# Nine gate/up chunk pairs of a feed-forward layer with Strassen's seven products over half of their k-tiles

## The chip, the cores and the metric

The kernel runs on one core of one Trainium2 chip. The metric is the device time of one execution in microseconds; the time of a kernel is the median of its runs. A core has four compute engines that matter here, each with an instruction queue of its own that it works through in order: TensorE (PE in the profile, its weight loads PEld), VectorE (DVE), ScalarE (ACT) and GpSimd (POOL). SyncE (SP) issues the DMA transfers. TensorE reads SBUF and writes PSUM; VectorE and ScalarE read and write both.

## The reference

One decoder layer, 256 rows of 2048 columns, all in fp32:

```python
def swiglu(x, w_in, w_out):
    a, u = jnp.split(x @ w_in, 2, axis=-1)
    return (jax.nn.silu(a) * u) @ w_out

x = layer_norm(ALPHA * x + 0.5 * swiglu(x, ffn1_w_in[i], ffn1_w_out[i]), ln_g[i, 0], ln_b[i, 0])
z = x @ mix_w_in[i]
...
x = layer_norm(ALPHA * x + merged @ mix_w_out[i], ln_g[i, 1], ln_b[i, 1])
x = layer_norm(ALPHA * x + 0.5 * swiglu(x, ffn2_w_in[i], ffn2_w_out[i]), ln_g[i, 2], ln_b[i, 2])
ple = jax.nn.sigmoid(x @ ple_w_gate[i]) * (p[i] @ ple_w_proj[i])
x = layer_norm(ALPHA * x + ple, ln_g[i, 3], ln_b[i, 3])
```

`w_in` is 2048 x 11008: 5504 gate columns (a), then 5504 up columns (u). `w_out` is 5504 x 2048. Between the two feed-forward layers stands a mixer of a short convolution and a gated recurrence (`hgrn`), which the change doesn't touch.

## The kernel before, in words

**Matmuls in three passes.** TensorE works with operands in fp32r. To keep fp32 accuracy each operand is split into a high half (a cast to fp32r) and a low half (what the cast lost), and a product is the sum of three matmuls: high x high (L741), high x low of the weight (L742), low x high (L743). The activations are the stationary operand, in blocks of 128 x 128 (`xh`, `xl` for x; `gh`, `gl` for h); the weights stream as 128 x 512 (`wh`, `wl`). There are two row tiles (t = 0 and 1, 128 rows each), and 16 k-tiles of 128 in a contraction over 2048.

**Units and the ring of weights.** The work is a list of Units (L50): one column block of 512 of one weight matrix, its k-tiles grouped in twos (an element: two k-tiles of 512 columns), the elements grouped in blocks (SPLIT, two blocks of 4 elements for 16 k-tiles). For each block TensorE goes through the elements for t = 0 and then for t = 1. Every element of the whole kernel is in `plan` (L655), in the order of use. `weight_dma` (L668) loads it into a ring of four raw tiles through SP's queue; `weight_split` (L678) makes the high half on ScalarE (L687) and the low half on VectorE (L689, waiting for L687). The halves lie in a ring of six pairs (`NMAIN`), to which each stage can add more (`EXTRA`, L32: four in feed-forward stage 1, three in stage 2). A slot is free again when TensorE has used its element for t = 1. `feed` (L693) is called then and traces as many loads and splits as there is room for.

**What sets the order.** Each use of an element is a tick (L118). Work behind a Unit is deferred by a number of ticks (`defer`) and is traced between matmuls when its tick comes. The framework then schedules the traced program: each engine's final order is made by list scheduling with a simulated timeline, so it can differ from the order of the code; semaphores follow from data, and from the slots of the rings.

**A feed-forward stage** (`ffn`, L293) has three parts over the 5504 hidden columns: 16, 16 and 11 blocks of 128. In a part, each chunk of 512 columns (the last has 384) takes two Units, gate and up. Behind the gate, ScalarE makes SiLU (L305); behind the up, VectorE multiplies (L309) into `h`. h is then transposed, since the next matmul contracts over its columns: `to_stat_blocks` (L204) does it with 16 VectorE instructions on 32-row strips (L202), and `halves` (L182) makes its high half on ScalarE (L189) and its low half on VectorE (L190). At the end of a part four output Units (512 columns of `w_out` each, the part's k-tiles) add into x (L319, L322).

**Normalization.** `layer_norm` (L256) normalizes x, transposes it on TensorE (`transposed`, L176: four matmuls with the identity into one PSUM bank), applies scale and shift on ScalarE (L267) and splits it for the next stage. The same scale and shift are applied to x itself later, by VectorE, column by column at 40, 60, 80 and 100 ticks (L250, L251).

**PSUM** has eight banks: four for accumulators, two for transposes, two for the recurrence.

Of the kernel before, what the change touches and what calls it, by code (L numbers as in the profile page):

```python
# [31 lines left out]
EXTRA = {"ffn1": 4, "hgrn": 0, "merge": 0, "ffn2": 3, "ple": 1}  # L32
# [5 lines left out]
class Stat:  # L38
# [6 lines left out]
    def get(self, t, k):  # L45
        h, l = self.parts[t, k // 4]
        return h[:, k % 4, :], l[:, k % 4, :]


class Unit:  # L50


    def __init__(self, stat, w, row, nk, col, width, epi, split=SPLIT):
# [4 lines left out]
        for n in split:  # L58
            end = min(nk, k + n)
            if k < end:  # L60
                self.blocks.append([list(range(i, min(end, i + KG))) for i in range(k, end, KG)])
            k = end


@with_exitstack
def hybrid_layer(ctx: ExitStack, tc: tile.TileContext, x, p, ln_g, ln_b, ffn1_w_in, ffn1_w_out, mix_w_in,
# [15 lines left out]
    region = {}  # L82

    def open_region(kind):
# [4 lines left out]
        region["kind"] = kind  # L89
        region["pool"] = region["ctx"].enter_context(tc.tile_pool(name=kind, bufs=1, side="left", reuse_waits="tile"))  # L90

# [3 lines left out]
    ps_a = pool("ps_a", 4, space=PSUM)  # L95
    ps_t = pool("ps_t", 2, space=PSUM)
    ps_h = pool("ps_h", 2, space=PSUM)
# [78 lines left out]
    def transposed(src, nb):  # L176
        tp = ps_t.tile([P, CC], F32, tag="tp", name="tp")
# [4 lines left out]
    def halves(stat, t, g, src, nb, tag):  # L182

        where, bufs = (region["pool"], 4) if tag == "m" else (op, 8)
# [19 lines left out]
    def to_stat_blocks(stat, t, g, src, nb, tag):  # L204
        y = rtile([P, 4, P], F32, tag="hT", name="hT", bufs=2)
        turn_blocks(y, src, nb)
        halves(stat, t, g, y[:, :nb, :].rearrange("p a b -> p (a b)"), nb, tag)

# [47 lines left out]
    def layer_norm(t, i, scale, stat):  # L256
# [3 lines left out]
        def operand(c, xc):  # L260
            y = st.tile([P, CC], F32, tag="silu", name="y", bufs=2)
            tp = transposed(xc, 4)
# [6 lines left out]
            halves(stat, t, c, y, 4, "x")  # L269

        for c in range(4):
# [21 lines left out]
    def ffn(xs, w_in, w_out, ln_i, nxt):  # L293
        parts = [(0, 16), (16, 16), (32, 11)]
        for pi, (k0, nk) in enumerate(parts):
            g = Stat()
            ff0 = k0 * P
            ncols = nk * P
            for ci, c0 in enumerate(range(0, ncols, CC)):
                w = min(CC, ncols - c0)  # L300
                silu = {}

                def epi_a(t, acc, silu=silu, w=w):
                    silu[t] = st.tile([P, CC], F32, tag="silu", name="silu", bufs=2)
                    nc.scalar.activation(silu[t][:, :w], acc, AF.Silu)  # L305

                def epi_u(t, acc, silu=silu, w=w, ci=ci, g=g):
                    h = st.tile([P, CC], F32, tag="h", name="h", bufs=3)
                    nc.vector.tensor_tensor(out=h[:, :w], in0=silu[t][:, :w], in1=acc, op=ALU.mult)  # L309
                    defer(2, lambda: to_stat_blocks(g, t, ci, h, w // P, "g"))  # L310

                units.append(Unit(xs, w_in, 0, 16, ff0 + c0, w, epi_a, split=(LONG if ln_i else EARLY) if pi + ci == 0 else SPLIT))
                units.append(Unit(xs, w_in, 0, 16, DFF + ff0 + c0, w, epi_u))
            for c in range(4):
                def epi_o(t, acc, c=c, pi=pi):
                    settle(c)
                    xc = xt[t][:, c * CC : (c + 1) * CC]
                    if pi == 0:
                        nc.vector.scalar_tensor_tensor(out=xc, in0=xc, scalar=2.0 * ALPHA, in1=acc,  # L319
                                                       op0=ALU.mult, op1=ALU.add)  # L320
                    else:
                        nc.vector.tensor_tensor(out=xc, in0=xc, in1=acc, op=ALU.add)  # L322
                    if pi == 2:
                        ln_stat(t, c)
                        if c == 3:
                            layer_norm(t, ln_i, 0.5, nxt)
# [454 lines left out]
```

## Time and profile before

| | |
|---|---|
| Median of 3 runs | 2254.53 us (2253.58 to 2255.19) |
| The profiled execution | 2255.39 us |
| Its span, from the first to the last instruction | 2253.7 us |
| Granted TensorE clock, mean | 0.998 |
| DMA | 429.99 MB, mean 191 GB/s |

All numbers of the trace come from the one profiled execution. A group of instructions is shown as line, engine, operation, output<-inputs, shapes and count, then busy time and mean ns of one, then the idle time of the engine just before them and what ended it. A timeline row has start, duration and the instructions. TensorE's matmuls overlap, so the time that one takes of the engine is the spacing of starts, not its duration. Feed-forward stage 1 runs until about 713 us, the recurrence stage and the merging follow, and feed-forward stage 2 lies between about 1420 and 2135 us.

### The profile page before, as it was taken

How to read it: one execution, taken by the hardware profiler on the slowest of the kernel's cores; microseconds unless marked ns; L12 is line 12 of the kernel's file. 1: busy time of each engine (PE TensorE's matmuls, PEld its weight loads, DVE VectorE, ACT ScalarE, POOL GpSimd, SP SyncE). 2: the span in 40 equal slices, each digit the busy share in tenths (PEclk: the TensorE clock that was granted, in tenths of full speed). 3: DMA queues.
4: the chain of work that ended last, by engine and by line, in shares of the span. 5: the costliest groups of instructions: out<-in, count | busy, mean ns of one | idle time of the engine just before them, and what ended most of it. 6: DMA issues, size and time to landing. Idle time of an engine off the chain costs nothing.

```text
span 2253.7 us, 27116 instructions
## 1 busy us (share of the span) xinstructions
PE 2228.8 (99%) x10154; PEld 1858.6 (82%) x10154; DVE 1498.5 (66%) x2214; ACT 1002.6 (44%) x1168; POOL 9.8 (0%) x32
## 2 busy tenths in 40 slices
PE   9999999999999999999999999999999999999997
PEld 7888888888897888888888888788888888889886
DVE  6776466764685578557555875678745767467667
ACT  6443344433445544434444443644434444344473
POOL 1000000000000000000000000000000000000000
PEclk9999999999999999999999999999999999999999
DMA  8566655566564555554555665566665655655574
GB/s 287 187 203 197 197 186 192 183 207 203 164 197 145 185 181 171 182 180 150 187 187 187 198 199 191 169 214 205 214 199 184 196 192 195 198 190 178 163 242 148
DMA packets 225335, 429.99 MB, mean 191 GB/s; under 512 B 13740, under 2 KB 22452, under 8 KB 225204
## 3 DMA queue, kind: packets, MB, share of 16 engines
q1 hardware_dynamic: 225204, 428.27, 58.7%
q8 instruction: 79, 1.29, 0.2%
q14 instruction: 52, 0.43, 0.1%
HBM read 426.12 MB, written 2.10 MB: 190 GB/s over the span
## 4 chain that ended last, share of the span: by engine, by line
PE 96%; DVE 2%; DMA 1%; ACT 0%; issue 0%; SPq 0%; DVEq 0%; ACTq 0%
PE acc L741 31%; PE acc L743 31%; PE acc L742 31%; PE gp L424 1%; PE tp L179 1%; DVE wl L689 1%; DMA raw<-in_ple_w_gate_dram 0%; DVE x L273 0%; DVE x L286 0%; DVE x L287 0%; DMA x<-in_x_dram 0%; PE dg L394 0%; ACT y L267 0%; DVE xl L190 0%; ACT L224 0%
## 5 line engine op out<-in xcount | busy, mean ns | idle before, releaser
L689 DVE TENSOR_TENSOR wl<-raw,wh 128x1024 fp32r<-128x1024 f32 (+2 forms) x804 | 958.9, 1207 | 500.8 <-ACT wh L687 466.0
L687 ACT CAST wh<-raw 128x1024 fp32r<-128x1024 f32 (+2 forms) x804 | 831.2, 1038 | 1003.8 <-PE acc L743 862.9
L743 PE MATMUL acc<-wh,xl 128*128 128x512 f32 (+1 forms) x2240 | 865.8, 387 | 2.6 <-DVE xl L190 2.6
L741 PE MATMUL acc<-wh,xh 128*128 128x512 f32 (+1 forms) x2240 | 865.5, 388 | 2.2 <-ACT xh L189 2.2
L742 PE MATMUL acc<-wl,xh 128*128 128x512 f32 (+1 forms) x2240 | 865.2, 387 | 0.0
L743 PEld LDWEIGHTS acc<-wh,xl 128*128 128x128 f32 x2240 | 420.8, 188 | 86.3 <-DVE xl L190 4.5
L741 PEld LDWEIGHTS acc<-wh,xh 128*128 128x128 f32 x2240 | 421.0, 188 | 84.1 <-ACT xh L189 3.2
L742 PEld LDWEIGHTS acc<-wl,xh 128*128 128x128 f32 x2240 | 420.9, 188 | 82.1 <-DVE wl L689 0.5
L743 PE MATMUL acc<-wh,gl 128*128 128x512 f32 x880 | 342.5, 389 | 0.0
L741 PE MATMUL acc<-wh,gh 128*128 128x512 f32 x880 | 342.4, 389 | 0.0
L742 PE MATMUL acc<-wl,gh 128*128 128x512 f32 x880 | 342.2, 389 | 0.0
L202 DVE STREAM_TRANSPOSE hT<-h 32x128 f32<-32x128 f32 (+1 forms) x704 | 210.8, 299 | 9.8
L743 PEld LDWEIGHTS acc<-wh,gl 128*128 128x128 f32 x880 | 165.2, 188 | 34.3
L742 PEld LDWEIGHTS acc<-wl,gh 128*128 128x128 f32 x880 | 165.2, 188 | 34.2
L741 PEld LDWEIGHTS acc<-wh,gh 128*128 128x128 f32 x880 | 165.2, 188 | 34.0
L309 DVE TENSOR_TENSOR h<-silu,acc 128x512 f32<-128x512 f32 (+1 forms) x44 | 29.6, 672 | 53.5 <-PE acc L743 53.5
L189 ACT CAST gh<-hT 128x512 fp32r<-128x512 f32 (+1 forms) x48 | 29.5, 614 | 62.8 <-DVE hT L202 62.8
L305 ACT ACTIVATE silu<-acc 128x512 f32<-128x512 f32 (+1 forms) x44 | 25.8, 586 | 52.2 <-PE acc L743 52.2
L322 DVE TENSOR_TENSOR x<-x,acc 128x512 f32<-128x512 f32 x32 | 21.8, 683 | 31.6 <-PE acc L743 31.6
L267 ACT ACTIVATE y<-tp,gbT 128x128 f32<-128x128 f32 x96 | 36.0, 466 | 7.6 <-PE tp L179 4.5
L190 DVE TENSOR_TENSOR gl<-hT,gh 128x512 fp32r<-128x512 f32 (+1 forms) x48 | 32.3, 674 | 0.0
L250 DVE TENSOR_TENSOR x<-x,gb 128x512 f32<-128x512 f32 x24 | 16.4, 723 | 22.0 <-DMA gb<-in_ln_g_dram 22.0
(147 smaller groups left out, 668.6 us busy)
## 6 DMA issues: line engine op xcount, KB each, us to landing
raw<-in_ffn_w_in_dram SPq DMA_DIRECT2D x320, 512.0 KB, 4.7
raw<-in_mix_w_in_dram SPq DMA_DIRECT2D x176, 512.0 KB, 4.6
raw<-in_ffn_w_out_dram SPq DMA_DIRECT2D x168, 512.0 KB, 5.3
raw<-in_mix_w_out_dram SPq DMA_DIRECT2D x32, 512.0 KB, 5.2
raw<-in_ple_w_gate_dram SPq DMA_DIRECT2D x32, 512.0 KB, 5.0
raw<-in_ffn_w_in_dram SPq DMA_DIRECT2D x32, 384.0 KB, 3.9
raw<-in_branch_w_conv_dram SPq DMA_DIRECT2D x16, 512.0 KB, 4.7
raw<-in_branch_w_hgrn_dram SPq DMA_DIRECT2D x16, 512.0 KB, 4.6
```

The costliest lines, as they stand in the source:

```text
L179: state["turned"] = nc.tensor.transpose(tp[:, i * P : (i + 1) * P], src[:, i * P : (i + 1) * P], ident).ins
L189: nc.scalar.copy(hf, src)
L190: nc.vector.tensor_tensor(out=lf, in0=src, in1=hf.bitcast(F32), op=ALU.subtract)
L202: nc.vector.transpose(dst[32 * b : 32 * b + 32, :nb, 32 * q : 32 * q + 32], cols[32 * q : 32 * q + 32, :, b, :])
L267: nc.scalar.activation(y[:, a * P : (a + 1) * P], tp[:, a * P : (a + 1) * P], AF.Identity, bias=gbT[:, 48 + k : 49 + k], scale=gbT[:, k : ...
L305: nc.scalar.activation(silu[t][:, :w], acc, AF.Silu)
L309: nc.vector.tensor_tensor(out=h[:, :w], in0=silu[t][:, :w], in1=acc, op=ALU.mult)
L687: nc.scalar.copy(h[:, :n, :w], raw[:, :n, :w])
L689: nc.vector.tensor_tensor(out=l[:, :n, :w], in0=raw[:, :n, :w], in1=h[:, :n, :w].bitcast(F32), op=ALU.subtract)
L741: nc.tensor.matmul(acc, sh, wh[:, a, : u.width], start=first, stop=False)
L742: nc.tensor.matmul(acc, sh, wl[:, a, : u.width], start=False, stop=False)
L743: nc.tensor.matmul(acc, sl, wh[:, a, : u.width], start=False, stop=last)
```

## The change

It touches the feed-forward stages, the weight rings and the PSUM banks.

**Quads.** Chunks 1 to 9 (nine pairs of gate and up blocks, 512 columns each) are no longer two Units but one Quad. Over the k-tiles 0 to 7 the four blocks (k-tiles `lo` and `hi`, gate and up columns: raw tiles 11, 12, 21, 22) are multiplied with the two row tiles by Strassen's scheme in Winograd's form: seven products instead of eight, with four sums of weight tiles (t1 to t4, made on VectorE in place on the raw tiles before they are split) and four sums of the stationary side (s1 to s4, made once per stage). It is done in two steps of 2 + 2 k-tiles. The k-tiles 8 to 15 stay plain (elements a0, a1 for gate and u0, u1 for up) and are accumulated into the same seven PSUM banks p1 to p7; for this the up columns' first product uses a stationary difference d of the two row tiles. In each step 11 elements are split, where two Units had 8 for the same columns. `after` combines the banks on VectorE and ScalarE: two copies, five additions and subtractions for the up columns, and for each row tile an addition, SiLU and a product.

**Rings.** The raw tiles of the seven products come through a second ring of five tiles (`sraw`, in a pool of its own), the rest through the old one of four. `EXTRA` is 0 in both feed-forward stages, so the ring of split weights has six slots. The cast on ScalarE may be traced one element ahead of the split.

**Order.** The hidden columns are now in five parts (two chunks each, the last has three), and the output Units of a part stand between the chunks of the next: two behind each of its first two chunks. So chunks 1 and 2 follow each other, chunk 2 is followed by two output Units, and so on; chunk 0 and the 384 columns of chunk 10 stay Units, and four output Units of 11 k-tiles end the stage.

**h** is transposed on TensorE (`to_stat`), three ticks after its product, through one PSUM bank. In the feed-forward stages PSUM is divided in seven banks for accumulators and one for transposes; elsewhere as before. The unsplit transposed x of k-tiles 0 to 15 is kept until the stationary sums are made.

```diff
-EXTRA = {"ffn1": 4, "hgrn": 0, "merge": 0, "ffn2": 3, "ple": 1}
+EXTRA = {"ffn1": 0, "hgrn": 0, "merge": 0, "ffn2": 0, "ple": 1}
+NSRAW = 5
+BANKS = {"ffn1": (7, 1, 0), "ffn2": (7, 1, 0)}
...
+class Quad:
...
+        for s in range(2):
+            lo, hi = (2 * s, 2 * s + 1), (4 + 2 * s, 5 + 2 * s)
+            n0, n1 = (8 + 4 * s, 9 + 4 * s), (10 + 4 * s, 11 + 4 * s)
+            k11, k12, k21, k22 = ((self, s, n) for n in ("11", "12", "21", "22"))
+            step = {
+                "11": dict(src=k11, use=[("p1", 0, lo)]),
+                "t1": dict(src=k11, add=k12, use=[("p5", "s1", lo)]),
+                "22": dict(src=k22, use=[("p3", "s4", lo)]),
+                "t3": dict(src=k12, add=k22, use=[("p7", "s3", lo)], free=[k12]),
+                "t2": dict(src=k11, add=k22, use=[("p6", "s2", lo)], drop=[k22]),
+                "21": dict(src=k21, use=[("p2", 0, hi)]),
+                "t4": dict(src=k11, add=k21, use=[("p4", 1, hi)], drop=[k21], free=[k11]),
+            }
+            for n, ks in (("a0", n0), ("a1", n1)):
+                step[n] = dict(load=[(ks, 0)], use=[("p2", 0, ks), ("p4", 1, ks)])
+            for n, ks in (("u0", n0), ("u1", n1)):
+                step[n] = dict(load=[(ks, 1)], use=[("p3", "d", ks), ("p5", 1, ks)])
+            step["11"]["sums"] = [(k12, lo, 1), (k22, hi, 1), (k21, hi, 0), (k11, lo, 0)]
+            order = "11 u0 t1 u1 22 t3 a0 t2 a1 21 t4".split()
...
-            defer((6 if t == 0 else 4) + c, lambda c=c, xc=xc: operand(c, xc))
+            defer((4 if t else 7 if stat is x2 else 6) + c, lambda c=c, xc=xc: operand(c, xc))
...
+        def turn(g, t, ci, h, w):
+            defer(3, lambda: to_stat(g, t, ci, h, w // P, "g"))
...
+                def after(el, ps):
+                    if el["step"] == 0:
+                        return
+                    if el["name"] == "11":
+                        made["c11"] = work("h")
+                        nc.scalar.copy(made["c11"], ps["p1"])
+                    elif el["name"] == "22":
+                        made["c12"] = work("silu")
+                        nc.scalar.copy(made["c12"], ps["p3"])
+                        both(made["c12"], made["c12"], ps["p5"], ALU.add)
+                    elif el["name"] == "t2":
+                        made["e"], made["c22"] = work("silu"), work("h")
+                        e = made["e"]
+                        both(e, made["c11"], ps["p6"], ALU.add)
+                        both(made["c12"], made["c12"], e, ALU.subtract)
+                        both(e, e, ps["p7"], ALU.add)
+                        both(made["c22"], ps["p5"], e, ALU.subtract)
+                    elif el["name"] == "21":
+                        h = made["c11"]
+                        both(h, h, ps["p2"], ALU.add)
+                        nc.scalar.activation(h, h, AF.Silu)
+                        both(h, h, made["c12"], ALU.mult)
+                        turn(g, 0, ci, h, CC)
+                    elif el["name"] == "t4":
+                        e = made["e"]
+                        both(e, e, ps["p4"], ALU.add)
+                        nc.scalar.activation(e, e, AF.Silu)
+                        both(e, e, made["c22"], ALU.mult)
+                        turn(g, 1, ci, e, CC)
...
+        for pi, chunks in enumerate(parts):
+            for ci, ch in enumerate(chunks):
+                in_units(ch, gs[pi], ci)
+                if pi and ci < 2:
+                    out_unit(pi - 1, 2 * ci)
+                    out_unit(pi - 1, 2 * ci + 1)
+        for c in range(4):
+            out_unit(len(parts) - 1, c)
...
+    def weight_cast():
+        el = plan[cur["cast"]]
+        n, w, where = el["n"], el["w"], el["where"]
+        raw = raws[el["src"]]
+        if "add" in el:
+            nc.vector.tensor_tensor(out=raw[:, :n, :w], in0=raw[:, :n, :w], in1=raws[el["add"]][:, :n, :w], op=ALU.add)
+            drop(el.get("drop", ()))
...
+        nc.scalar.copy(h[:, :n, :w], raw[:, :n, :w])
...
     def feed():
         while True:
+            if may_load("sraw"):
+                weight_dma("sraw")
+            elif may_load("raw"):
                 weight_dma()
+            elif castable():
+                weight_cast()
+            elif cur["split"] < cur["cast"]:
                 weight_split()
             else:
                 return
...
+        for el in u.els:
+            for bank, t, ks in el["use"]:
+                tick()
...
+                for a, k in enumerate(ks):
+                    left[bank] -= 1
+                    passes(ps[bank], u.stat, t, k, gi, a, first and a == 0, left[bank] == 0)
+            consumed(gi)
+            u.after(el, ps)
...
+    def first_operand(t, c):
+        tp = transposed(xt[t][:, c * CC : (c + 1) * CC], 4, "a")
+        halves(x0, t, c, tp, 4, "x")
+        nc.scalar.copy(plain_tile(t, c), tp)
+        if (t, c) == (NT - 1, 3):
+            sums(x0)
```

`src` is the raw tile that an element is split from, `add` the one that is added to it first; `use` names bank, stationary operand and k-tiles; `drop` and `free` say which raw tiles are given back after the sum and after the split. `passes` issues the three matmuls per k-tile as before, and `consumed` frees the element's slot and calls `feed`.

More of the change, by code (lines that the diff above doesn't have):

```diff
@@ L82, in hybrid_layer @@
     region = {}
+    held = {}
     def open_region(kind):
@@ L293, in ffn @@
     def ffn(xs, w_in, w_out, ln_i, nxt):
[L294 to L326, printed above, removed]
-                units.append(Unit(g, w_out, ff0, nk, c * CC, CC, epi_o, split=(12,) if (pi == 2 and c == 3) else SPLIT))
@@ L725, in hybrid_layer @@
             feed()
[L726 to L750 removed]
     drain()
     region.pop("ctx").close()
+    region.pop("psum").close()
 _INS = ['x', 'p', 'ln_g', 'ln_b', 'ffn1_w_in', 'ffn1_w_out', 'mix_w_in', 'conv_w', 'hg_lower_bound', 'hg_norm_w',
```

280 lines of the change are left out of this document (214 added, 66 removed).

## The prediction

> **What bounds the kernel now.** I read the page first, then the groups of instructions kept apart by shape, the waits, and the timelines of TensorE and VectorE inside the first feed-forward stage.
>
> ```profile
> span 2253.7 us, 27116 instructions
> ...
> PE 2228.8 (99%) x10154; PEld 1858.6 (82%) x10154; DVE 1498.5 (66%) x2214; ACT 1002.6 (44%) x1168; POOL 9.8 (0%) x32
> ...
> PE 96%; DVE 2%; DMA 1%; ACT 0%; issue 0%; SPq 0%; DVEq 0%; ACTq 0%
> ```
>
> TensorE is busy for 99% of the span and makes up 96% of the chain that ended last. A shorter time needs fewer TensorE instructions, or shorter ones; VectorE, at 66%, has room on average. The average hides where the change puts its work, so the stage counts:
>
> ```profile
> 45.00:713.00 668.00, 668.00 (x2993) 559.00 (x2992) 442.34 (x682) 279.18 (x294) 0.96 (x1) 1.00 0.59 192
> ...
> 840.00:860.00 20.00, 20.00 (x108) 17.13 (x106) 18.06 (x24) 7.87 (x9) 0.00 (x0) 1.00 0.53 163
> ...
> 2000.00:2010.00 10.00, 10.00 (x46) 8.29 (x45) 9.80 (x20) 3.86 (x5) 0.00 (x0) 1.00 0.63 204
> ```
>
> These are answers by stretch: width, then PE, PEld, DVE, ACT, POOL, the granted clock, DMA share, GB/s. The first is feed-forward stage 1: TensorE has no gap in 668 us, the clock is 1.00, VectorE takes 442 us. The other two show VectorE at 90% and 98% for 20 and 10 us while TensorE still has no gap. High VectorE load for a while isn't by itself a stall.
>
> A matmul's mean duration (390 ns) is not its price, since matmuls overlap. The price is the spacing of their starts:
>
> ```profile
> 150.17 0.39 PE L741 MATMUL acc<-wh,xh 128*128 128x512 f32 x1
> ...
> 165.81 0.39 PE L741 MATMUL acc<-wh,xh 128*128 128x512 f32 x1
> ```
>
> Between these two lie 23 rounds of L741, L742, L743: 15.64 us / 69 = 0.2267 us for each.
>
> **Matmuls removed.** A gate/up chunk pair now takes 2 column blocks x 2 row tiles x 16 k-tiles x 3 passes = 192 matmuls. In a Quad, each of its two steps has 7 products of 2 k-tiles, and 4 plain elements of 2 k-tiles used twice: (14 + 16) x 3 = 90, so 180. Nine pairs in two stages: 18 x 12 = 216 fewer, x 0.2267 = **-49.0 us**, all of it on TensorE's path. The output units keep their 43 k-tiles in all, so their matmul count doesn't move.
>
> **Transposes added to TensorE.** h went through VectorE (L202); now it takes four TensorE transposes per 512 columns. The stage after shows what such a group costs:
>
> ```profile
> 768.62 0.39 PE L741 MATMUL acc<-wh,xh 128*128 128x512 f32 x1
> 768.85 0.60 PE L179 MATMUL tp<-ident,s 128*128 128x128 f32 x4
> 769.20 0.48 PE L742 MATMUL acc<-wl,xh 128*128 128x512 f32 x1
> 769.51 0.40 PE L743 MATMUL acc<-wh,xl 128*128 128x512 f32 x1
> 769.75 0.40 PE L741 MATMUL acc<-wh,xh 128*128 128x512 f32 x1
> ```
>
> From L741 to the next L741 pass 1.13 us instead of 3 x 0.2267 = 0.68: a group costs 0.45 us. There are 2 stages x 2 tiles x 11 chunks = 44 groups: **+19.8 us**. The bounds are 0.25 us (if the two matmuls behind it hadn't been slowed) and 4 x 0.272 = 1.09 us (the rows' full duration, below), or 11 to 48 us; I take 0.45 because it is the same operation between the same matmuls. The Trainium skill ("TensorE: Matmul & The Clock Gate", Part 4: PE-mode transpose) speaks against the edit: about 275 ns per transpose in a kernel's context, and the array's full clock isn't held by transposes. By that price the term would be 172 x 0.275 = 47 us and eat nearly all of the gain. The row agrees with the duration but not with the price, since four overlap into 0.45 us, and the granted clock in the stretch 840 to 860 us, which holds small TensorE products, is 1.00.
>
> **VectorE and ScalarE, per Quad.** Rows by shape, and the spacing when they stand back to back:
>
> ```profile
> L689 DVE TENSOR_TENSOR wl<-raw,wh 128x1024 fp32r<-128x1024 f32 x764 | 924.3, 1223 | 482.2 <-ACT wh L687 447.6
> ...
> L687 ACT CAST wh<-raw 128x1024 fp32r<-128x1024 f32 x764 | 799.9, 1050 | 956.2 <-PE acc L743 822.2 <-DMA raw<-in_ffn_w_in_dram 57.4 <-DMA raw<-in_ffn_w_out_dram 26.2
> ...
> L189 ACT CAST gh<-hT 128x512 fp32r<-128x512 f32 x44 | 27.4, 623 | 57.1 <-DVE hT L202 57.1
> ...
> L305 ACT ACTIVATE silu<-acc 128x512 f32<-128x512 f32 x40 | 23.8, 596 | 50.2 <-PE acc L743 50.1
> ...
> L179 PE MATMUL tp<-ident,s 128*128 128x128 f32 x32 | 4.8, 272 | 0.0
> ...
> L389 DVE TENSOR_TENSOR kb<-qT,kT 128x1024 f32<-128x1024 f32 x2 | 2.5, 1226 | 9.8 <-ACT qT L506 9.8
> ...
> L558 ACT COPY b<-acc 128x512 f32<-128x512 f32 x4 | 2.3, 585 | 6.6 <-PE acc L743 6.6
> ```
> ```profile
> 143.93 3.50 DVE L689 TENSOR_TENSOR wl<-raw,wh 128x1024 fp32r<-128x1024 f32 x3
> 147.34 0.68 DVE L309 TENSOR_TENSOR h<-silu,acc 128x512 f32<-128x512 f32 x1
> 147.94 0.68 DVE L190 TENSOR_TENSOR gl<-hT,gh 128x512 fp32r<-128x512 f32 x1
> 148.54 1.22 DVE L689 TENSOR_TENSOR wl<-raw,wh 128x1024 fp32r<-128x1024 f32 x1
> 149.68 5.04 DVE L202 STREAM_TRANSPOSE hT<-h 32x128 f32<-32x128 f32 x16
> ```
>
> Three splits take 3.50 us, so one more costs (3.50 - 1.22)/2 = 1.14; a 512-wide operation costs 0.60 (147.34 to 147.94 to 148.54). A weight sum is the L389 shape (1226 ns against the split's 1223), so also 1.14. A pair before: 16 splits, two products, two times 16 transposes and a low half = 18.2 + 1.2 + 11.3 = 30.7 us of VectorE under 192 x 0.2267 = 43.5 of TensorE. A Quad: 22 splits (25.1), 8 sums (9.1), 9 combining operations (5.4), two low halves (1.2) = **40.8 us**, under 40.8 + 0.9 of TensorE. ScalarE has 22 x 1.05 + 2 x 0.585 + 2 x 0.596 + 2 x 0.623 = 26.7 us. So a Quad alone leaves VectorE nothing. The two output units put behind it bring 8 splits and 4 additions, 11.5 us, under 96 x 0.2267 = 21.8: together 52.3 us of VectorE under 63.5.
>
> What carries work from one to the other is the ring of six split weights; the sums need no ring slot, only their raw tiles, so they can be done early as well. I count from a Quad's start at full TensorE speed (1.36 us for an element used once, 2.72 for one used twice; a step is 20.4). Its first five elements were split while the output unit ran. From there each slot frees when the element six before it ends, and 1.05 + 1.14 us later the next is ready: for the fourth weight sum of the step (element t4) at about 11.7 us, needed at 19.0. The tightest is the next step's first tile, which can only be loaded once that sum has freed a buffer (five buffers in the second ring). The transfer needs:
>
> ```profile
> raw<-in_ffn_w_in_dram SPq DMA_DIRECT2D x320, 512.0 KB, 4.7
> ```
> ```profile
> SPq L674 <- DVE wl L689: 1695.4, 767, 17.5
> ```
>
> The sum ends between 7.5 and 8.9 us, the tile lands 4.7 us later, at 13.6 at the latest, and is split by 15.9; TensorE wants it at 20.4. The margin is 4.5 us. These transfers go through SP's one queue, which already spends 1695 us waiting for splits to free buffers; behind a waiting one stand the raw tiles of elements that are needed later, so this costs nothing while the margin stands.
>
> Two places are tighter. Pairs 1 and 2 follow each other with no output unit between: 81.6 us of VectorE under 83.4. In the second stage the scale-and-shift of the previous normalization falls among them, three of four columns:
>
> ```profile
> 820.39 1.28 DVE L251 TENSOR_TENSOR x<-x,gb 128x512 f32<-128x512 f32 x2
> ...
> 850.72 1.30 DVE L250 TENSOR_TENSOR x<-x,gb 128x512 f32<-128x512 f32 x2 [1.84 <-DMA gb<-in_ln_g_dram]
> ```
>
> That is 3 x 2.6 = 7.8 us more, 6 too much before the ring's store (six elements, some 8 us). I take 3 us there, and 0.2 us for each of the other 16 Quads, where a chain from product over SiLU to transpose ends late: together **+6 us**, from 0 to 18 (1 us a Quad).
>
> Three waits are new. ScalarE's cast of a summed tile waits for the sum; behind it in ScalarE's queue stand the next casts, the SiLUs and the cast of h. TensorE's transposes wait for h, and the next unit's matmuls stand behind them. With one PSUM bank for transposes instead of two, the second group waits until the first is cast and its low half taken (0.62 + 0.60); an element of 1.36 us lies between the two groups, so I put that at nothing, 1 us a Quad (in the 18 us) if VectorE is late.
>
> **The rest.** The second stage's first operands come one tick later: +1.4 us at most, taken. The copies at the start (8 x 0.585 us of ScalarE) lie beside loading of x, and the sums of the stationary side (12 VectorE operations, 7 us) under the first pair, which leaves 43.5 - 19.4: nothing, or 5 us if the cover were gone. The 32 extra additions of the output units are in the counts above. Fewer ring slots (6 for 10 and 9) is what the stage at 840 to 860 us has already.
>
> **Sum.** The profiled execution took 2255.4 us, 1.7 of it outside the span, and 0.9 above the median of the runs, 2254.5. 2255.4 - 49.0 + 19.8 + 6 + 1.4 = 2233.6; less 0.9, **2232.7 us**, 1.0% faster. About 0.2% (4.5 us) is what can be told from no change.
>
> **Rivals.**
> *VectorE becomes the bound in each Quad* (slower). The place is the weight sums: sum, then ScalarE's cast, then split, on the same tile. If VectorE stands idle for the cast, that is 8 x (1.05 + 0.08 of signalling) = 9.0 us, and a Quad needs 49.8. Less what was done ahead (6 x 1.14 and two sums with their idle time, 11.4), plus the next unit's first four (4.6): 43.0 against 41.7, 1.3 us late. In that order the fourth sum comes at 11.6, the next step's tile lands at 16.4, and VectorE, done at 12.7 + 1.14 with it, loses another 3.7 us. 5.0 x 18 = 90 us: 2316. It decides from (49.0 - 19.8 - 1.4)/18 = 1.5 us a Quad. For it: VectorE already waits 447.6 us for casts (row L689). Against it: the order on VectorE isn't the written one. gl (L190) is written straight behind the 16 transposes, yet at 143.93 to 147.94 three splits and a product were put into its wait for ScalarE. The same filling can be done with sums.
> *Transposes at full price*: 0.272 each in the open, 172 x 0.272 = 46.8: 2255.4 - 49.0 + 46.8 + 1.4 - 0.9 = 2253.7, no change. The row at 768.85 speaks against it. It is the price that the page of the Trainium skill named above would give.
> *Better*: no stalls, and transposes at 0.25: 2255.4 - 49.0 + 11 + 0.5 - 0.9 = 2217.
>
> **How the numbers follow.** Forecast 0.64 (2221, with no stall, no late tick and a group at 0.35, to 2250, with 18 us of stall and 5 at the start; 0.02 of it within 0.2%), VectorE bound 0.26 (0.03 of it within, where the stall is near 1.5 us a Quad), transposes at full price 0.06 (0.05 within), better 0.04. So faster 0.66, same 0.10, slower 0.24. The range goes to 2290, about 3.5 us of stall a Quad, which leaves out the upper half of the VectorE case and most of the better one.
>
> **What would show it.** Right: 9,384 weight matmuls for 9,600; 172 transposes of h at about 0.45 us per four; no group of PE with more than some 10 us idle before it; VectorE near 85% in the feed-forward stages and idle in the output units. Wrong: TensorE waiting for weight splits or for h by more than 1.5 us a Quad, VectorE above 95% in a Quad, or casts that wait for the second ring's transfers.

## The result, and the profile after

The changed kernel takes 2266.09 us (median, 2265.55 to 2266.74) where the kernel before took 2254.68 in the same comparison: a ratio of 1.0051, 95% interval 1.0034 to 1.0069. It is slower by 0.5%, where 1.0% faster was forecast. The profiled execution took 2265.55 us, its span is 2263.8 us and its mean granted clock 0.992.

The page of the changed kernel, the same three lines as before:

```profile
span 2263.8 us, 26974 instructions
...
PE 2215.5 (98%) x10110; PEld 1842.7 (81%) x10110; DVE 1682.0 (74%) x1944; ACT 1130.7 (50%) x1331; POOL 10.0 (0%) x32
...
PE 89%; DVE 4%; DMA 3%; ACT 2%; issue 1%; SPq 0%; DVEq 0%; ACTq 0%
```

TensorE's busy time fell by 13 us, and the span still grew by 10. In the chain that ended last TensorE fell from 96% to 89%; VectorE, DMA and ScalarE took its place. TensorE now waits. The stretches say where (columns as in the prediction):

```profile
320.00:340.00 20.00, 20.00 (x90) 16.59 (x89) 19.96 (x21) 12.73 (x14) 0.00 (x0) 1.00 0.76 244
...
120.00:140.00 20.00, 17.96 (x78) 13.75 (x77) 15.65 (x15) 12.51 (x14) 0.00 (x0) 1.00 0.52 164
...
1520.00:1540.00 20.00, 17.63 (x74) 13.00 (x73) 17.64 (x20) 11.53 (x14) 0.00 (x0) 1.00 0.50 135
1540.00:1560.00 20.00, 16.71 (x59) 12.49 (x58) 14.68 (x16) 5.76 (x7) 0.00 (x0) 0.83 0.59 186
...
1400.00:1440.00 40.00, 31.39 (x143) 26.26 (x142) 23.94 (x40) 19.24 (x34) 0.00 (x0) 0.87 0.49 158
```

The first stretch lies in a later Quad: VectorE at 19.96 us of 20, TensorE without a gap. The next three lie in the second Quad of stage 1 and of stage 2 (the end of the first Quad included). There TensorE has gaps while VectorE is *less* busy than in the first; so VectorE isn't simply full, something stops it too. The last is the end of the merging stage.

To count the losses I went over TensorE's rows and added up every spacing of starts beyond what the instruction needs: 0.2267 us for 512 columns, 0.173 for 384, 0.088 for a 128-wide transpose. This is worked out from the rows, not a view of the profile. By place, in us:

| TensorE's loss | before | after |
|---|---|---|
| Start (0 to 40 us) | 6.9 | 11.4 |
| Quads 1 and 2, stage 1 | 0 | 4.5 |
| End of feed-forward stage 1 | 6.6 | 10.3 |
| Recurrence and merging | 6.4 | 6.4 |
| End of merging | 7.0 | 12.9 |
| Quads 1 and 2, stage 2 | 0 | 13.2 |
| Rest of the feed-forward stages | 0 | 4.5 |
| End of feed-forward stage 2 | 1.9 | 7.9 |
| Sum over all spacings | 28.9 | 71.9 |

The rows of the second column make 71.1; the other 0.8 us are a few nanoseconds each in many spacings. The 4.5 us in the rest of the stages are transposes slowing the two matmuls behind them, which the +19.8 us of the prediction hold already. The remaining growth is 71.9 - 28.9 - 4.5 = 38.5 us, and -49.0 + 19.8 + 38.5 = +9.3; behind TensorE's last matmul it is 0.9 longer too, and the span grew by 10.1. So the removed matmuls and the added transposes came as forecast, and three kinds of places ate the gain: Quads 1 and 2 (17.7 us), the stage ends (15.6) and the start (4.5).

Not all of this is waiting. During and behind the waits the granted clock is 0.50 for a while: from 713.5 to 720.2 us, 1427 to 1437, 1553.2 to 1559.9 and 2150.5 to 2153.8, and in the kernel before only behind TensorE's last matmul. The TensorE instructions that start there need about 9 us at the spacings above; as they take twice that, some 9 of the 38.5 us (an estimate from these rows) are the slower clock that comes with the waits.

**Quads 1 and 2.** ScalarE's timeline, then VectorE's, then TensorE's, in stage 2:

```profile
1519.16 1.05 ACT L884 CAST wh<-sraw 128x1024 fp32r<-128x1024 f32 x1 [3.36 <-DVE sraw L878]
1523.80 1.05 ACT L884 CAST wh<-sraw 128x1024 fp32r<-128x1024 f32 x1 [3.58 <-DMA sraw<-in_ffn_w_in_dram]
...
1552.33 1.04 ACT L884 CAST wh<-sraw 128x1024 fp32r<-128x1024 f32 x1 [3.25 <-DMA sraw<-in_ffn_w_in_dram]
```
```profile
1517.86 1.21 DVE L878 TENSOR_TENSOR sraw<-sraw 128x1024 f32<-128x1024 f32 x1
...
1524.87 1.22 DVE L895 TENSOR_TENSOR wl<-sraw,wh 128x1024 fp32r<-128x1024 f32 x1 [2.08 <-ACT wh L884]
...
1546.24 1.22 DVE L878 TENSOR_TENSOR sraw<-sraw 128x1024 f32<-128x1024 f32 x1
...
1553.41 1.22 DVE L895 TENSOR_TENSOR wl<-sraw,wh 128x1024 fp32r<-128x1024 f32 x1 [2.96 <-ACT wh L884]
```
```profile
1553.43 0.80 PE L951 MATMUL p<-wh,xh 128*128 128x512 f32 x1 [2.10 <-ACT wh L884]
```

The fourth sum of a step (L878) ends at 1519.07 us, and only then can the next step's first tile be loaded. The cast of that tile, at the head of ScalarE's queue, waits 3.58 us for the transfer; VectorE, which has to split the tile, stands idle for 2.08 us behind it. One step later the fourth sum ends at 1547.46 us, the cast waits 3.25, VectorE stands idle for 2.96, and TensorE waits 2.10 us for the cast. This is the chain that the prediction's first rival described, fourth sum to next step's tile. In later Quads it is there too, but TensorE has no gap. The row of the waits:

```profile
ACT wh L884 <- DMA sraw<-in_ffn_w_in_dram: 82.9, 20, 5.2
```

Twenty casts waited 82.9 us in all. Most of it cost TensorE nothing: in the fourth Quad of stage 1 the fourth sum ends 9.1 us into its step (235.06 to 244.19) and TensorE goes on without a gap. In the second Quad of stage 1 it ends 18.0 us into the step, in stage 2 22.6. The later Quads have two output units behind them, in which VectorE can catch up.

**Stage ends.** The normalization at the end of merging, on VectorE, in the kernel before and in the changed one:

```profile
1421.33 1.92 DVE L273 TENSOR_SCALAR x<-x,mv,r 128x512 f32<-128x512 f32 x4
1423.16 3.49 DVE L689 TENSOR_TENSOR wl<-raw,wh 128x1024 fp32r<-128x1024 f32 x3
```
```profile
1419.91 1.92 DVE L378 TENSOR_SCALAR x<-x,mv,r 128x512 f32<-128x512 f32 x4
1421.74 4.62 DVE L895 TENSOR_TENSOR wl<-raw,wh 128x1024 fp32r<-128x1024 f32 x4
```

The code holds the next two weight splits back until the normalization of x is through (`gate["lo"]`), to bring the normalization forward. Behind it now stand four splits instead of three, which is all raw tiles there are. The changed kernel's ScalarE, and TensorE:

```profile
1426.71 1.05 ACT L884 CAST wh<-raw 128x1024 fp32r<-128x1024 f32 x1 [4.64 <-DMA raw<-in_ffn_w_in_dram]
1429.32 1.04 ACT L884 CAST wh<-raw 128x1024 fp32r<-128x1024 f32 x1 [1.57 <-DMA raw<-in_ffn_w_in_dram]
1430.27 1.50 ACT L370 ACTIVATE yT<-tp,gbT 128x128 f32<-128x128 f32 x4
```
```profile
1432.47 0.80 PE L951 MATMUL acc<-wh,xh 128*128 128x512 f32 x1 [8.61 <-ACT xh L242]
1433.06 0.63 PE L952 MATMUL acc<-wl,xh 128*128 128x512 f32 x1
```

With every raw tile held, the next transfer starts only when the first of the four splits is done; two casts ahead of the operand wait 4.64 and 1.57 us for it, and TensorE, which needs the operand, waits 8.61. The kernel before has the same hold. There ScalarE takes the operand ahead of the cast that follows:

```profile
1423.97 1.51 ACT L267 ACTIVATE y<-tp,gbT 128x128 f32<-128x128 f32 x4 [1.43 <-PE tp L179]
1425.36 1.05 ACT L687 CAST wh<-raw 128x1024 fp32r<-128x1024 f32 x1
```

Six slots alone don't make this loss, as a run of the kernel before with six slots shows below (7.4 us there). Whether the cast that may be traced one element ahead, the later tick or something else put more casts ahead of the operand, no run tells apart.

### The profile page after: what moved, and what is told of

Same layout as the page of the kernel before. It is cut to its first block, busy times and chain, and to the rows that moved or that the text cites. A ratio compares the mean times of both kernels' runs of the same rounds, so it can differ in the third digit from the quotient of the medians.

```text
span 2263.8 us, 26974 instructions
## 1 busy us (share of the span) xinstructions
PE 2215.5 (98%) x10110; PEld 1842.7 (81%) x10110; DVE 1682.0 (74%) x1944; ACT 1130.7 (50%) x1331; POOL 10.0 (0%) x32
## 4 chain that ended last, share of the span: by engine, by line
PE 89%; DVE 4%; DMA 3%; ACT 2%; issue 1%; SPq 0%; DVEq 0%; ACTq 0%
PE acc L951 20%; PE acc L953 20%; PE acc L952 20%; PE p L952 9%; PE p L953 9%; PE p L951 9%; DVE wl L895 2%; PE tp L232 2%; DMA sraw<-in_ffn_w_in_dram 1%; PE gp L587 1%; DVE sraw L878 1%; ACT wh L884 1%; ACT yT L370 1%; DMA raw<-in_ple_w_gate_dram 0%; DMA raw<-in_ffn_w_in_dram 0%
## 5 line engine op out<-in xcount | busy, mean ns | idle before, releaser
L951 PE MATMUL acc<-wh,xh 128*128 128x512 f32 (+1 forms) x1088 | 418.9, 388 | 13.4 <-ACT xh L242 9.0
L953 PE MATMUL acc<-wh,xl 128*128 128x512 f32 (+1 forms) x1088 | 419.3, 386 | 0.1
L952 PE MATMUL acc<-wl,xh 128*128 128x512 f32 (+1 forms) x1088 | 418.2, 385 | 0.0
L884 ACT CAST wh<-sraw 128x1024 fp32r<-128x1024 f32 x252 | 262.7, 1049 | 286.9 <-DVE sraw L878 89.5
L895 DVE TENSOR_TENSOR wl<-sraw,wh 128x1024 fp32r<-128x1024 f32 x252 | 306.2, 1221 | 109.2 <-ACT wh L884 105.5
L951 PE MATMUL p<-wh,xh 128*128 128x512 f32 x648 | 251.7, 391 | 3.9 <-ACT wh L884 3.9
L952 PE MATMUL p<-wl,xh 128*128 128x512 f32 x648 | 253.3, 391 | 0.8 <-DVE wl L895 0.8
L953 PE MATMUL p<-wh,xl 128*128 128x512 f32 x648 | 253.1, 391 | 0.0
L951 PEld LDWEIGHTS acc<-wh,xh 128*128 128x128 f32 x1088 | 205.4, 189 | 50.8 <-ACT xh L242 9.6
L953 PEld LDWEIGHTS acc<-wh,xl 128*128 128x128 f32 x1088 | 205.2, 189 | 38.8 <-DVE xl L243 1.4
L878 DVE TENSOR_TENSOR sraw<-sraw 128x1024 f32<-128x1024 f32 x144 | 175.4, 1218 | 0.6
```

Source lines behind the costliest of these rows:

```text
L878: nc.vector.tensor_tensor(out=raw[:, :n, :w], in0=raw[:, :n, :w], in1=raws[el["add"]][:, :n, :w], op=ALU.add)
L884: nc.scalar.copy(h[:, :n, :w], raw[:, :n, :w])
L895: nc.vector.tensor_tensor(out=l[:, :n, :w], in0=raw[:, :n, :w], in1=h[:, :n, :w].bitcast(F32), op=ALU.subtract)
L951: nc.tensor.matmul(acc, sh, wh[:, a, :n], start=first, stop=False)
L952: nc.tensor.matmul(acc, sh, wl[:, a, :n], start=False, stop=False)
L953: nc.tensor.matmul(acc, sl, wh[:, a, :n], start=False, stop=last)
```

## The experiments

All ratios are to the kernel before, timed beside each run.

**A plain chunk 1.** Undoes one part: chunk 1 is two Units again, so that no two Quads follow each other without output units.

```diff
-            if w == CC and ch > 0:
+            if w == CC and ch > 1:
```

> Chunk 1 stays two Units, so the first Quad of a stage is chunk 2 and has output Units behind it: eight Quads per stage instead of nine, 24 matmuls more in all (+5.4 us). In the changed kernel TensorE's starts lose 4.4 us (stage 1, 100 to 140 us) and 13.0 us (stage 2, 1520 to 1580 us) beyond a spacing of 0.2267 us, all in the first two Quads. Theory A, the two Quads without output Units between them run VectorE into its limit: both losses go, -17.4 + 5.4 = -12 us, about 2254 us. Rival B, the loss is that of any Quad near the start of a stage (six slots in the ring, the second ring filling up): the loss moves to chunks 2 and 3 and the time rises by 5 us, to 2271 us.

Measured: 2252.16 us, ratio 0.9985 (0.9976 to 0.9994): 13.9 us faster than the change, though it has 24 matmuls (5.4 us) more. The stretch that held the loss in stage 2:

```profile
1500.00:1600.00 100.00, 100.00 (x450) 82.72 (x449) 86.11 (x91) 50.68 (x55) 0.00 (x0) 1.00 0.66 205
```

No gap is left, and the loss in the two places falls from 17.7 to 0.8 us. The place is settled; why the pair stalls isn't yet.

**The scale-and-shift later.** My own cause for Quads 1 and 2 was VectorE's extra 7.8 us of scale-and-shift. Here it comes behind them.

```diff
-                defer(40 + 20 * c, lambda c=c: affine_rows(i, c, range(NT)))
+                defer(88 + 4 * c if i == 1 else 40 + 20 * c, lambda c=c: affine_rows(i, c, range(NT)))
```

> The scale and shift of the second normalization is applied at ticks 92 to 104 of feed-forward stage 2 instead of 44 to 104, behind the first two Quads instead of among them. Theory A (VectorE at its limit in the first two Quads) says that three of its four columns, 7.8 us of VectorE, make the difference between the 13.0 us lost in stage 2 and the 4.4 us lost in stage 1: about -8 us, 2258 us. Rival, the two Quads lose that much by themselves, through late transfers into the second ring: within 2 us of 2266 us.

Measured: 2264.45 us, 1.0042 (1.0027 to 1.0057). Two neighbouring stretches of this kernel:

```profile
1500.00:1600.00 100.00, 97.23 (x429) 78.42 (x428) 88.18 (x95) 52.24 (x59) 0.00 (x0) 1.00 0.61 185
1600.00:1700.00 100.00, 96.89 (x417) 77.83 (x416) 87.70 (x87) 51.78 (x56) 0.00 (x0) 0.98 0.68 212
```

The loss in Quads 1 and 2 of stage 2 fell from 13.2 to 4.0 us, about what stage 1 loses there (4.5), where that work is absent too. But some 8 us came up in Quad 3 (1593 to 1640 us), where the work now lies, although output units follow that Quad. So in this ring the work costs its time where it meets a Quad, and moving it doesn't remove the loss; the time fell by 1.6 us where I had expected 8.

**A ring of its own for tile 11.** The next step's first tile gets two buffers of its own instead of waiting for one of five shared buffers to come free; the other three tiles share three. The memory is the same.

```diff
-NSRAW = 5
+NSRAW = {"s11": 2, "sraw": 3}
...
-                    loads["sraw"].append((key, kind, u.w, ks[0] * P, 2, u.cols[n], u.width))
+                    loads["s11" if key[2] == "11" else "sraw"].append((key, kind, u.w, ks[0] * P, 2, u.cols[n], u.width))
...
+            if may_load("s11"):
+                weight_dma("s11")
+            elif may_load("sraw"):
+                weight_dma("sraw")
```

> The changed kernel with the five buffers of the second ring divided: two for the first tile of a step (11), three for 12, 22 and 21, so that the next step's first tile can be loaded a whole step early instead of after the last weight sum. Same work, same VectorE load. Theory A1, in the first two Quads the stall is the transfer of that tile behind a late sum (ScalarE waits 82.9 us in all for the second ring's transfers): the 17.7 us lost in the first two Quads of the stages fall below 6, about 2254 us. Rival A2, it is the amount of VectorE work there, whatever the transfers do: less than 4 us change, 2262 to 2266 us.

Measured: 2247.43 us, 0.9965 (0.9953 to 0.9977): 18.7 us faster than the change, faster than the kernel before, and with all 18 Quads. First the group of casts (line, shapes, count, busy, mean, idle before), then two stretches:

```profile
L887 ACT CAST wh<-sraw 128x1024 fp32r<-128x1024 f32 x252 | 264.1, 1050 | 184.5 <-PE p L958 112.9 <-PE acc L958 33.5 <-issue 21.3
```
```profile
1520.00:1540.00 20.00, 20.00 (x94) 16.57 (x93) 20.00 (x23) 9.80 (x12) 0.00 (x0) 1.00 0.63 191
1540.00:1560.00 20.00, 20.00 (x90) 16.53 (x89) 18.88 (x21) 13.17 (x15) 0.00 (x0) 1.00 0.61 203
```

The DMA is gone from the releasers of these casts; they now wait for TensorE to free a slot, which is what a weight that is ready early looks like. VectorE is busier than in the change (20.00 and 18.88 against 17.64 and 14.68) and TensorE has no gap, with the scale-and-shift still among these Quads. So VectorE had the room. It was kept idle by the transfer, and that was the cause of the 17.7 us: 1.5 are left. The edit also lets tile 11 be loaded ahead of the other tiles whenever it has a buffer; what the buffers and what that order did isn't told apart.

**Six slots for the kernel before.** One part of the change alone: `EXTRA` is 0 in the feed-forward stages, nothing else.

```diff
-EXTRA = {"ffn1": 4, "hgrn": 0, "merge": 0, "ffn2": 3, "ple": 1}
+EXTRA = {"ffn1": 0, "hgrn": 0, "merge": 0, "ffn2": 0, "ple": 1}
```

> The kernel before with EXTRA 0 in both feed-forward stages and nothing else changed. At the three normalizations that end a stage the changed kernel loses 4.3, 6.2 and 6.0 us more than the kernel before. Theory C, with six slots that all serve any stage, more weight casts of the next stage are put ahead of the normalized operand, and ScalarE waits there for their transfers: this kernel loses 10 to 16 us there, about 2267 us. Rival D, the loss at these places comes from the new division of PSUM, the tick added to the second stage's operands and the separate cast and split: this kernel stays within 3 us of the kernel before, 2255 us.

Measured: 2263.97 us, 1.0041 (1.0027 to 1.0055). VectorE at the end of stage 1:

```profile
714.06 1.92 DVE L273 TENSOR_SCALAR x<-x,mv,r 128x512 f32<-128x512 f32 x4
715.90 4.63 DVE L689 TENSOR_TENSOR wl<-raw,wh 128x1024 fp32r<-128x1024 f32 x4
```

The four splits behind the normalization are here without any Quad, and the loss there grows from 6.6 to 11.2 us, at the end of stage 2 from 1.9 to 4.7. Another 2.2 us lie inside stage 2 (1500 to 1600 us), where the kernel before loses nothing: TensorE waits 0.82 and 0.57 us there for a split on VectorE. I had put the fewer slots at nothing; in this kernel they cost 8.7 us (9.8 in the profiled execution, to which the losses belong). The end of merging is hardly worse (7.0 to 7.4), so its 5.9 us in the change come of something more, and the three stage ends together lose 7.8 us more, less than the 10 to 16 that I had expected.

**The order of the PSUM banks.** In the changed kernel TensorE waits 4.41 us at the end of stage 1 for a PSUM bank that an addition into x still reads. Here the pools are laid out in another order, so that the next stage's accumulators fall on other banks.

```diff
-            for n, b in zip("ath", banks):
+            for n, b in sorted(zip("ath", banks), key=lambda e: banks[2] and "hta".index(e[0])):
```

> The changed kernel; only, outside the feed-forward stages the three kinds of PSUM banks are laid out in the reverse order, so that the first accumulators of the next stage lie in banks 4 to 7 and not in bank 0, which the last accumulator of stage 1 used. Theory: at the end of stage 1 TensorE waits 4.4 us for the addition that empties bank 0, and 4 us return, about 2262 us. Rival: it waits for the normalized operand or for the weights anyway, and less than 1.5 us returns, 2265 us.

Measured: 2264.99 us, 1.0042 (1.0028 to 1.0056). TensorE at that place:

```profile
716.56 0.80 PE L953 MATMUL acc<-wh,xl 128*128 128x512 f32 x1 [3.42 <-DVE xl L243]
```

The wait for the bank is gone, and in its place TensorE waits 3.42 us for the low half of x, which stands on VectorE behind the same four splits. The bank was the wait that came last, not the cause.

**One transpose bank at the start.** In the change all eight transposes of x go before the first product, since seven accumulator banks let them. Here they use the one transpose bank.

```diff
-        tp = transposed(xt[t][:, c * CC : (c + 1) * CC], 4, "a")
+        tp = transposed(xt[t][:, c * CC : (c + 1) * CC], 4, "t")
```

> The changed kernel with the transposes of the very first operands in the single PSUM bank for transposes instead of the seven accumulator banks. In the changed kernel all eight groups of transposes stand ahead of the first matmul and wait for x one after the other; the first matmul starts at 16.1 us instead of 7.4, and TensorE loses 4.9 us more up to 20 us. Theory E, seven free banks let the transposes be put in front: with one bank matmuls come between them again and 3 to 5 us return, about 2262 us. Rival, the extra copies on ScalarE (eight of 0.585 us) hold up the start: no change, 2266 us.

Measured: 2268.08 us, 1.0057 (1.0042 to 1.0072). The loss at the start rose from 11.4 to 14.0 us; it moved behind 20 us, where the single bank is held by the cast, the low half and the new copy of x. No gain, and the start's cause was left open by this run.

**Casts held at a stage's end.** No more than three of the next stage's elements may be cast until the stage is open.

```diff
+                and (el["nth"] < 3 or el["stage"] in (units[0][0], "merge")
+                     or el["stage"] == region["kind"] and state["tick"] >= region["opened"] + 2))
```

> The changed kernel; only, of the next stage's elements no more than three are cast before the stage opens, and the fourth not before two ticks in it, so that the normalized operand is traced first. Theory C (the six-slot kernel lost 4.6 and 2.8 us at the first and last of the three normalizations, with four casts and four splits ahead of the operand, and then ScalarE waiting for a transfer): some 6 us return there, and at the middle one up to 5.9 us, where ScalarE waits 4.6 and 1.6 us for transfers ahead of the operand: 2254 to 2260 us. Rival: the normalization's own chain sets the end there, less than 3 us returns.

Measured: 2265.20 us, 1.0047 (1.0031 to 1.0062). ScalarE at the end of merging:

```profile
1418.44 2.93 ACT L886 CAST wh<-raw 128x1024 fp32r<-128x1024 f32 x3
1426.00 1.04 ACT L886 CAST wh<-raw 128x1024 fp32r<-128x1024 f32 x1 [4.63 <-DMA raw<-in_ffn_w_in_dram]
```

The order on the engine came out as in the change, so the run tells nothing about the cause.

**Three edits.** The plain chunk 1, the order of banks and the held casts together.

> Chunk 1 as two Units, the reversed order of PSUM banks and the held casts together. If the three are independent, the gains add up: 2252.2 us with the first alone, less 4 and less 6 to 12: 2236 to 2242 us, 0.6 to 0.8% below the kernel before. If the two at the normalizations remove the same wait, 2245 us.

Measured: 2252.38 us, 0.9987 (0.9978 to 0.9995), as the plain chunk alone. The other two add nothing.

**No splits held behind the normalization.** On top of the own ring:

```diff
-                gate["lo"] = norm.ins, 2
+                gate["lo"] = norm.ins, 0
```

> The kernel with the own ring for tile 11 (2247.4 us), without the rule that holds two weight splits behind the normalization of x at the end of a stage. That kernel's TensorE loses 10.3, 12.1 and 8.8 us at the three stage ends, where the kernel before loses 5.7, 7.0 and 1.9. Theory H: the splits held behind the normalization give back their raw tiles late, the transfers of the next tiles start late, and ScalarE's casts then wait for them ahead of the operand. Without the rule the splits run in VectorE's idle time ahead of the normalization, the casts no longer wait 3 to 5 us for raw tiles, and the three losses fall by 8 to 15 us: 2232 to 2240 us. Rival R: the six slots of split weights, not the raw tiles, set what is ready at a stage end; then nothing is won, and splits that stand ahead of the normalization delay it by up to 1.2 us each: 2247 to 2252 us.

Measured: 2239.81 us, 0.9928 (0.9912 to 0.9944), 7.6 us less than the own ring alone. VectorE, ScalarE and TensorE at the end of merging:

```profile
1411.92 1.23 DVE L898 TENSOR_TENSOR wl<-raw,wh 128x1024 fp32r<-128x1024 f32 x1 [0.48 <-ACT wh L887]
...
1417.98 1.91 DVE L380 TENSOR_SCALAR x<-x,mv,r 128x512 f32<-128x512 f32 x4
```
```profile
1416.88 1.05 ACT L887 CAST wh<-raw 128x1024 fp32r<-128x1024 f32 x1 [0.64 <-DMA raw<-in_ffn_w_in_dram]
```
```profile
1422.53 0.80 PE L956 MATMUL acc<-wh,xh 128*128 128x512 f32 x1 [3.29 <-ACT xh L242]
```

With the own ring alone the cast is this:

```profile
1422.67 1.04 ACT L887 CAST wh<-raw 128x1024 fp32r<-128x1024 f32 x1 [4.64 <-DMA raw<-in_ffn_w_in_dram]
```

Four splits now stand ahead of the normalization, which comes 7.05 us behind the collected statistics (1410.93 us) instead of 3.15; but the raw tiles come free early, the cast waits 0.64 instead of 4.64, and TensorE 3.29 instead of 8.18. The loss there falls from 12.1 (own ring) to 7.7 us. At the ends of the two feed-forward stages it falls only from 10.4 to 8.7 and from 8.8 to 8.0. In the changed order of ScalarE the hold explains the end of merging (7.0 us before); at the other two it is a small part.

**The start's transposes in turn.** On top of the own ring; column group c at tick 2c, still in the accumulator banks.

```diff
-            defer(0, lambda t=t, c=c: first_operand(t, c))
+            defer(2 * c, lambda t=t, c=c: first_operand(t, c))
```

> The kernel with the own ring for tile 11 (2247.4 us), with the transposes of x at the start spread over the ticks (column group c at tick 2c) and still in the accumulator banks. Theory S: TensorE's loss at the start, 11.5 us against 7.0 before, comes of eight transposes that all stand ahead of the first product, each pair waiting for its part of x; with products between them the first product starts near 8 us and the loss falls to about 7: 2243 us. Rival A: the parts of x and the weights come one after the other through one queue and the matmuls would be starved a little later; the loss only moves, as it did with one transpose bank: 2247 to 2250 us.

Measured: 2243.64 us, 0.9947 (0.9933 to 0.9961), 3.8 us less than the own ring alone; the loss at the start is 7.1 us. TensorE's first rows in the changed kernel and in this one:

```profile
12.99 3.68 PE L232 MATMUL tp<-ident,x 128*128 128x128 f32 x16 [0.92 <-DMA x<-in_x_dram]
16.32 0.78 PE L951 MATMUL acc<-wh,xh 128*128 128x512 f32 x1
```
```profile
7.73 0.78 PE L956 MATMUL acc<-wh,xh 128*128 128x512 f32 x1
```

The first product starts at 7.73 us instead of 16.32. The transposes that stood ahead of it, each waiting for its part of x, were the start's cause.

**Own ring, no hold, start in turn.**

> Own ring for tile 11, no splits held behind the normalization, and the start's transposes in turn. If theories H and S hold and add up: 2228 to 2236 us. If only H: 2232 to 2240. If neither: 2247 to 2252, like the own ring alone.

Measured: 2238.64 us, 0.9926 (0.9912 to 0.9940): 0.7% faster than the kernel before and 1.2% faster than the change, the lowest time of these kernels, if hardly below the 2239.81 us without the start's edit. The two edits together bring 8.8 us where singly they brought 7.6 and 3.8: the end of stage 1 lost again here (10.2 us, against 8.7 without the start's edit). TensorE waits the same there (3.80 us for the normalized x, against 3.79), but behind the wait the granted clock is 0.50 for longer, from 703 to 713 us against 710.1 to 716.8. Why it lasts longer no run shows. This kernel's loss stands at 45.5 us; the ends of the two feed-forward stages (10.2 and 7.7, against 6.6 and 1.9 before) are what is left. The run of the kernel before with six slots shows 4.6 and 2.8 us of it. More slots weren't tried with the Quads.

## Why the prediction was wrong, point by point

**Matmuls removed: right.** The page's 10110 TensorE instructions are 10154 less 216 and plus 172, and later Quads run without a gap.

**Transposes: right.** TensorE in the changed kernel:

```profile
123.10 0.39 PE L953 MATMUL p<-wh,xl 128*128 128x512 f32 x1
123.33 0.60 PE L232 MATMUL tp<-ident,silu 128*128 128x128 f32 x4
123.69 0.48 PE L951 MATMUL p<-wh,xh 128*128 128x512 f32 x1
124.00 0.40 PE L952 MATMUL p<-wl,xh 128*128 128x512 f32 x1
124.24 0.40 PE L953 MATMUL p<-wh,xl 128*128 128x512 f32 x1
124.47 0.40 PE L951 MATMUL p<-wh,xh 128*128 128x512 f32 x1
```

From 123.10 to 124.47 are 1.37 us for four matmuls and one group, so the group costs 0.46 us (0.45 forecast). The 275 ns for each transpose of the Trainium skill ("TensorE: Matmul & The Clock Gate", Part 4) don't add up to a price here either.

**VectorE's work in a Quad: right. Its waits: nothing found in the later Quads.** The 144 sums (8 a Quad) and the 252 splits from the second ring (14 a Quad) came as counted. For each of the 16 later Quads I took 0.2 us of stall; beside the transposes' share nothing can be found, so that term was too dear. With the own ring VectorE stands at 20.00 of 20 us and TensorE doesn't wait.

**"The margin of 4.5 us": the step that failed first.** It was worked out for a VectorE that keeps pace, and then taken for all Quads: "this costs nothing while the margin stands". In Quads 1 and 2 it doesn't stand. I had the fourth sum end 7.5 to 8.9 us into a step, and the next step's tile land at 13.6 us at the latest. In the second Quad of stage 1 the sum ends at 18.0 us and the cast of the tile starts at 22.5, behind the 20.4 us at which TensorE wants the tile already split; in stage 2 it is 15.2 and 19.9 us in the first Quad's second step, then 22.6 and 27.4. I saw that the place was tight and gave it 3 us, as a matter of VectorE's work (81.6 under 83.4, and 6 of scale-and-shift too much); it cost 17.7, 4.5 of them in stage 1, where I had nothing but two times 0.2. Nor did I have a term for the clock: about 3 of the 13.2 us in stage 2 are matmuls at the granted 0.50 behind the waits. What I left out is that lateness feeds itself: a late fourth sum makes the transfer late, the cast waits for it at the head of ScalarE's queue, VectorE goes idle behind the cast, and the next sum is later still. Five shared buffers made that loop; two buffers of its own for one tile cut it. The rival had the mechanism and priced it in every Quad (5.0 us, 90 in all); TensorE loses by it in the second Quad of each stage alone, 4.5 and 13.2 us. What I had set against the rival, that other work fills VectorE's wait for a cast, didn't hold there: VectorE stood idle for 2.08 and 2.96 us.

**"The rest": nothing, or 5 us at the start.** The start cost 4.5 us, by the transposes and not by the copies that I had costed. "Fewer ring slots is what the stage at 840 to 860 us has already" was a bad comparison: a stage that runs steadily says nothing of a stage's end. The stage ends cost 15.6 us; with the slots alone the kernel before loses 7.8 us more at them. In the other half the hold has a part (with the own ring 4.4 us at the end of merging, 1.7 and 0.8 at the two others), and the rest stays open. The late tick of the second stage's operands (+1.4) lies in the end of merging and can't be told apart there.

By the terms of the prediction's sum: -49.0, +19.8, then 38.5 in place of 6 + 1.4, and 0.9 at the end.

## What to carry to other kernels

Work out the margin of a shared ring of buffers where the engine that frees it is latest, not where it keeps pace: a wait that goes round through a transfer and a queue in order starves the very engine that is short of time, and an idle gap on a nearly full engine is the sign of it. Buffers of its own for the tile on that loop cost no memory here and were worth 18.7 us, where moving VectorE's work brought 1.6. When a change takes buffers away, look at the ends of the stages as well as at their middle, and look there for rules of order that were set for the old number.

## What the runs showed of the hardware

In these traces a wait of TensorE can cost more than its length, since the granted clock falls to 0.50 during it or behind it. The wait of 8.61 us at the end of merging is one case; the stretch from 1420 to 1440 us shows it as a mean of 0.74:

```profile
1420.00:1440.00 20.00, 11.39 (x55) 9.67 (x54) 14.22 (x25) 11.70 (x26) 0.00 (x0) 0.74 0.48 158
```

In stage 2 the mean is 0.83 from 1540 to 1560 us, where the longest single wait is 2.10 us, though several stand close together (0.28, 0.76 and 2.10 us within six). The matmuls behind it start 0.43 us apart instead of 0.2267:

```profile
1555.39 0.63 PE L952 MATMUL p<-wl,xh 128*128 128x512 f32 x1
1555.82 0.63 PE L953 MATMUL p<-wh,xl 128*128 128x512 f32 x1
```

With the scale-and-shift later the longest single wait is 1.13 us (to 1618.41 us), and the clock is 0.50 from 1618.5 to 1621.8. The Trainium skill ("TensorE: Matmul & The Clock Gate", Part 1) gives an idle time of some 3.4 us as what halves the clock; the wait of 8.61 us agrees, and the other two show that shorter waits in a row can do it too.
